# The weight pieces of an up-projection move to GpSimd, its gating to VectorE, and a half's first pieces move ahead of an attention output

## The chip, the cores and the metric

One core of one Trainium2 chip runs the whole program. The metric is the device time of one execution in microseconds (us). TensorE (PE in the profile) multiplies matrices, VectorE (DVE), ScalarE (ACT) and GpSimd (POOL) work element by element, and SyncE (SP) issues nearly all DMA transfers in one queue.

## The reference

One layer of a hybrid encoder over 2048 tokens of width 1024: a token mixer, a cross-attention into a memory, and the feed-forward block that this change is about.

```python
x = x + hybrid_token_mixer(rmsnorm(x, norm_mix), ...)
x = x + mem_cross_attn(rmsnorm(x, norm_x), memn, x_wq, x_wkv, x_wo)
h = rmsnorm(x, norm_ffn)
gate, val = split(h @ w_up)                   # 1024 -> 2 x 2816
gate = causal_dwconv(gate, conv_w, conv_b)    # 3 taps over the tokens
x = x + (silu(gate) * val) @ w_down           # 2816 -> 1024
return rmsnorm(x, norm_final)
```

## The kernel before

Every float32 matrix operand is used as a pair, a rounded high part and the remainder as low part; a product is three matmuls for each 128 rows (high x high, high x low, low x high). `resplit(t_, eng, raw)` makes a pair: ScalarE copies the high part (L1331), then the engine `eng` subtracts to get the low part (L1332).

The mixer fills the first 1400 us or so and is not touched. The rest is the block `attn_ffn`. It takes the tokens in two halves of 1024, each half as two blocks (NB = 2) of TB = 512 tokens. For each half, `attention` runs the scores and then `attn_out` for o = 0 and o = 1. One call of `attn_out` loops over 8 output tiles d; each loads two weight tiles `wvo` (L1286) and the residual `x2` (L1341), runs 24 matmuls, adds the residual on VectorE (L1344), stores it (L1345), and sums its squares (L1220: with o = 0 on GpSimd, with o = 1 on VectorE). With o = 1 it also makes the seven activation operands that the up-projection wants, `11`, `21`, `22`, `t1` to `t4`; the low parts of `t2` and `22` and four subtractions for `t4` (L1375) are GpSimd's.

Then `ffn_up` loops over 22 column tiles f. Both blocks and both halves of the rows of a weight tile are multiplied by a scheme with seven products in place of eight; each product is 12 matmuls (L1446 to L1448), so that an f has 84. The seven weight pieces are `a11`, `s1`, `s2`, `a12`, `s3`, `s4`, `a22`. With half 0, `up_weights` makes them from two raw tiles (`wraw`, two `load_raw` of 512 KB, L96): four sums s1 to s4 (L1426, L1428, L1430, L1432) and seven `resplit`; each piece is also stored in `ws_dram` (L1435). With half 1 the seven pieces are loaded from `ws_dram` (L1411) and nothing is formed. The `s` pieces lie in a pool of 7 buffers (`KQ`), which the attention uses for `wvo`; the `a` pieces have buffers of their own.

The products end in PSUM. ScalarE copies three of them to SBUF (`kept`, L1452: p1, p5, u2, and with `u3` a fourth). `gate(b)`, once for each block, is the chain of one f: copy of two carried columns (L1473), addition (L1474, one operand in PSUM), multiplication by the row scale `bc3` (L1475), ScalarE's first tap (L1476), two taps (L1478), copy of the new carry (L1479), tanh (L1481, into `fth`), its product (L1482), and a second multiplication by `bc3` (L1483). `u3 += p5` is L1489. The last products, L1499, take `u3` for one block and a PSUM tile `pd` for the other. `bc3` comes out of `bcast_rstd`: TensorE sums squares (`ssps`, L1226), the reciprocal root goes over VectorE and GpSimd (L182, L183), TensorE spreads it (`bcB`, L1235). `ffn_down` follows.

The block is put in order by a scheduler that simulates time with prices of its own (`schedule_with_timeline_sim=True`, L1183); each engine then works its list in order. A changed line can therefore move others.

Of the kernel before, what the change touches and what calls it, by code (L numbers as in the profile page):

```python
# [13 lines left out]
F32 = mybir.dt.float32  # L14
# [7 lines left out]
P = 128  # L22
# [34 lines left out]
def tile_hybrid_encoder(ctx: ExitStack, tc: tile.TileContext, t_in: dict, out: bass.AP, stage: str = "all"):  # L57
# [1148 lines left out]
    def KQ(shape, name):  # L1206
        return kq.tile(list(shape), FR, tag="kq", name=name)
# [193 lines left out]
    fcar = [fcars[:, 4 * f:4 * f + 2] for f in range(NFF)]  # L1401
    def up_weights(hf, f):

        H = KT // 2
        pcs = {}

        def piece(i, name):
            pool = name[0] == "a"
            pcs[name] = wpool.tile([P, 2, H, P], FR, tag="whl", name="wa", bufs=WB) if pool else KQ((P, 2, H, P), "ws")
            if hf:  # L1410
                nc.sync.dma_start(pcs[name].bitcast(F32), ws_dram[f, i])  # L1411
            return pcs[name]

        order = ("a11", "s1", "s2", "a12", "s3", "s4", "a22")
        if hf:
            for i, name in enumerate(order):
                piece(i, name)
            return pcs
        rg, rv = load_raw(t_in["f_up"][f]), load_raw(t_in["f_up"][NFF + f])
        g1, g2, v1, v2 = rg[:, :H], rg[:, H:], rv[:, :H], rv[:, H:]  # L1420
        s1r, s2r, s3r, s4r = [t_[:, u] for t_ in [K4((P, 2, H, P), "sr", F32) for _ in range(2)] for u in range(2)]
        raws = dict(a11=g1, a12=g2, a22=v2, s1=s1r, s2=s2r, s3=s3r, s4=s4r)
        for i, name in enumerate(order):
            t_ = piece(i, name)
            if name == "s1":
                nc.gpsimd.tensor_tensor(s1r, v1, v2, ALU.add)  # L1426
            elif name == "s2":
                nc.vector.tensor_tensor(s2r, s1r, g1, ALU.subtract)  # L1428
            elif name == "s3":
                nc.vector.tensor_tensor(s3r, v1, g1, ALU.subtract)  # L1430
            elif name == "s4":
                nc.gpsimd.tensor_tensor(s4r, g2, s2r, ALU.subtract)  # L1432
            resplit(t_, nc.vector if name in ("s2", "s3") else nc.gpsimd, raws[name])
            if S > HALF:
                nc.sync.dma_start(ws_dram[f, i], t_.bitcast(F32))  # L1435
        return pcs

    def ffn_up(hf, st, B, early):

        H = KT // 2  # L1440
        for f in range(NFF):
            w = up_weights(hf, f)

            def prod(ps, a, b, more=False):
                for k in range(H):
# [24 lines left out]
            def gate(b):  # L1470
                u = us[:, b]
                gt_ = T((P, TB + 2), "gt_")
                nc.gpsimd.tensor_copy(gt_[:, 0:2], fcar[f])  # L1473
                nc.vector.tensor_tensor(gt_[:, 2:], (R, Z)[b], (p1, u2)[b], ALU.add)  # L1474
                nc.vector.tensor_tensor(gt_[:, 2:], gt_[:, 2:], st[b]["bc3"], ALU.mult)  # L1475
                nc.scalar.activation(u, gt_[:, 2:], AF.Identity, scale=V("fcw2", f), bias=V("fcb", f))  # L1476
                for tap in range(2):
                    nc.vector.scalar_tensor_tensor(u, gt_[:, tap:tap + TB], V(f"fcw{tap}", f), u, ALU.mult, ALU.add)  # L1478
                nc.gpsimd.tensor_copy(fcar[f], gt_[:, TB:TB + 2])  # L1479
                th = T(name="fth")  # L1480
                nc.scalar.activation(th, u, AF.Tanh, scale=0.5)  # L1481
                nc.vector.scalar_tensor_tensor(u, th, 1.0, u, ALU.add, ALU.mult)  # L1482
                nc.gpsimd.tensor_tensor(u, u, st[b]["bc3"], ALU.mult)  # L1483

            if f:
                gate(0)
            prod(X, "s3", "t3", True)
            u3 = kept(X, "u3")
            nc.gpsimd.tensor_tensor(u3, u3, p5, ALU.add)  # L1489
            prod(Z, "s4", "22", True)  # L1490
            if f == 0:
                prod(X, "a22", "t4", True)
# [195 lines left out]
```

## Time and profile before

| | |
|---|---|
| median of 3 runs (lowest to highest) | 3439.07 us (3436.12 to 3439.97) |
| the profiled execution, its span | 3434.74 us, 3433.0 us |
| TensorE busy | 3242.5 us, 94% |
| VectorE busy | 2038.0 us, 59% |
| ScalarE busy | 1300.0 us, 38% |
| GpSimd busy | 1283.5 us, 37% |
| mean granted TensorE clock | 0.979 |

The profile is one execution; busy shares are means over stages with different limits, so the stretches of the up-projection are read on their own. The up-projection of half 0 fills about 1697 to 2197 us, that of half 1 about 2740 to 3190 us.

### The profile page before, as it was taken

What the parts mean: (1) busy time and instruction counts of PE and PEld (TensorE: products, weight loads), DVE (VectorE), ACT (ScalarE), POOL (GpSimd) and SP (SyncE); (2) the same over time, 40 slices, a digit from 0 to 9 for tenths busy, and PEclk for the clock granted to TensorE, in tenths of its full rate; (3) what the DMA queues carried; (4) which work ended last, traced back from release to release, by engine and by line L of the source; (5) the groups of instructions that cost most, each with busy time, mean ns of one, the idle gap of its engine ahead of it and who ended that gap; (6) DMA issues with size and microseconds to landing.
All of it is one profiled execution on the core that took longest, in us unless ns stands there. A gap on an engine that the chain in (4) does not pass through costs nothing.

```text
span 3433.0 us, 48215 instructions
## 1 busy us (share of the span) xinstructions
PE 3242.5 (94%) x16860; PEld 2646.4 (77%) x16860; DVE 2038.0 (59%) x3942; ACT 1300.0 (38%) x2593; POOL 1283.5 (37%) x1318
## 2 busy tenths in 40 slices
PE   6999999999999989899889999899999999999998
PEld 4777787788778778688677777687888778888787
DVE  5887777777777785343487777723243454445321
ACT  5445433543443345432234344433322232223432
POOL 5333121211211123531277777755611132323543
PEclk9999999999999999999999999999999999999999
DMA  5555444544444447866566666754556766666552
GB/s 206 210 180 183 142 142 130 176 131 142 147 131 128 131 128 233 270 209 213 177 238 237 241 240 245 258 185 158 172 199 203 236 212 218 219 222 214 194 173 76
DMA packets 317299, 647.72 MB, mean 189 GB/s; under 512 B 89728, under 2 KB 121600, under 8 KB 317056
## 3 DMA queue, kind: packets, MB, share of 16 engines
q1 hardware_dynamic: 312832, 642.53, 55.7%
q8 instruction: 134, 2.20, 0.3%
q10 hardware_dynamic: 4224, 2.10, 0.2%
q14 instruction: 109, 0.89, 0.1%
HBM read 454.64 MB, written 189.86 MB: 188 GB/s over the span
## 4 chain that ended last, share of the span: by engine, by line
PE 55%; DVE 15%; DMA 9%; POOL 8%; issue 8%; ACT 4%; SPq 1%; POOLq 0%; DVEq 0%; ACTq 0%
PE pd L147 11%; PE pd L1446 4%; PE pd L1447 4%; PE pd L1448 4%; DMA x<-x_dram 4%; PE dps L1547 3%; PE dps L1545 3%; PE dps L1546 3%; PE qy L147 2%; PE pd L176 2%; PE pd L173 2%; PE pd L175 2%; PE sc L1298 2%; PE sc L1300 2%; PE sc L1299 2%
## 5 line engine op out<-in xcount | busy, mean ns | idle before, releaser
L147 PE MATMUL pd<-hA,whl 128*128 128x512 f32 x2976 | 814.5, 411 | 16.1 <-ACT whl L121 7.8
L147 PEld LDWEIGHTS pd<-hA,whl 128*128 128x128 f32 x2976 | 535.6, 192 | 119.9 <-ACT whl L121 9.4
L1446 PE MATMUL pd<-h,ws 128*128 128x512 f32 x704 | 280.7, 402 | 46.5 <-ACT u L1452 30.4
L1332 POOL TENSOR_TENSOR wd<-wdr,wd 128x512 fp32r<-128x512 f32 x176 | 238.3, 1363 | 186.6 <-ACT wd L1331 186.5
L1545 PE MATMUL dps<-act,wd 128*128 128x512 f32 x704 | 275.8, 392 | 7.2 <-DVE x L1569 3.8
L1448 PE MATMUL pd<-h,ws 128*128 128x512 f32 x704 | 280.9, 400 | 0.8 <-POOL ws L1332 0.8
L1447 PE MATMUL pd<-h,ws 128*128 128x512 f32 x704 | 280.6, 399 | 0.0
L1546 PE MATMUL dps<-act,wd 128*128 128x512 f32 x704 | 275.4, 391 | 0.0
L124 POOL TENSOR_TENSOR whl<-wraw,whl 128x512 fp32r<-128x512 f32 x137 | 187.2, 1377 | 235.4 <-ACT whl L121 226.7
L1547 PE MATMUL dps<-act,wd 128*128 128x512 f32 x704 | 270.6, 392 | 4.6 <-POOL wd L1332 4.6
L1446 PE MATMUL pd<-h,wa 128*128 128x512 f32 x528 | 207.3, 396 | 9.6 <-ACT u L1452 9.6
L1447 PE MATMUL pd<-h,wa 128*128 128x512 f32 x528 | 207.1, 392 | 0.0
L1448 PE MATMUL pd<-h,wa 128*128 128x512 f32 x528 | 207.0, 392 | 0.0
L1446 PEld LDWEIGHTS pd<-h,ws 128*128 128x128 f32 x704 | 135.8, 193 | 83.5 <-ACT u L1452 38.0
L1331 ACT CAST wd<-wdr 128x512 fp32r<-128x512 f32 x176 | 107.7, 619 | 186.3 <-PE dps L1547 127.4
L1483 POOL TENSOR_TENSOR fu<-fu,bcs 128x512 f32<-128x512 f32 x88 | 132.2, 1502 | 102.3 <-DVE fu L1482 92.2
L1448 PEld LDWEIGHTS pd<-h,ws 128*128 128x128 f32 x704 | 135.8, 193 | 33.2 <-POOL ws L1332 4.6
L1545 PEld LDWEIGHTS dps<-act,wd 128*128 128x128 f32 x704 | 132.9, 189 | 36.2 <-ACT wd L1331 4.3
L1547 PEld LDWEIGHTS dps<-act,wd 128*128 128x128 f32 x704 | 132.5, 189 | 33.8 <-POOL wd L1332 6.3
L1447 PEld LDWEIGHTS pd<-h,ws 128*128 128x128 f32 x704 | 135.9, 193 | 28.5 <-DVE h L1332 0.4
L1546 PEld LDWEIGHTS dps<-act,wd 128*128 128x128 f32 x704 | 133.0, 189 | 27.7
L1332 DVE TENSOR_TENSOR act<-act 128x512 fp32r<-128x512 f32 x88 | 73.7, 860 | 108.7 <-ACT act L1331 107.6
(1034 smaller groups left out, 7368.1 us busy)
## 6 DMA issues: line engine op xcount, KB each, us to landing
whl<-w_split SPq DMA_DIRECT2D x186, 512.0 KB
ws_dram<-ws SPq DMA_DIRECT2D x88, 512.0 KB
wdr<-f_down SPq DMA_DIRECT2D x176, 256.0 KB
ws<-ws_dram SPq DMA_DIRECT2D x88, 512.0 KB
ws_dram<-wa SPq DMA_DIRECT2D x66, 512.0 KB
wa<-ws_dram SPq DMA_DIRECT2D x66, 512.0 KB
wqk<-qk_dram SPq DMA_DIRECT2D x64, 512.0 KB
wvo<-vo_dram SPq DMA_DIRECT2D x64, 512.0 KB
```

Of the source, the lines that this page charges most:

```text
L124: (nc.vector if dve else nc.gpsimd).tensor_tensor(t_[:, 1], r_, t_[:, 0].bitcast(F32), ALU.subtract)
L147: nc.tensor.matmul(out_, lhsT, rhs, **kw)
L173: nc.tensor.matmul(ps, hi[:, k % 4, :], a[:, 0, :n], start=(k == 0), stop=False)
L1331: nc.scalar.copy(t_[:, 0], raw)
L1332: eng.tensor_tensor(t_[:, 1], raw, t_[:, 0].bitcast(F32), ALU.subtract)
L1446: nc.tensor.matmul(ps, w[a][:, 0, k, :], B[b][k][:, 0, :], start=(k == 0 and not more), stop=False, skip_group_check=True)
L1447: nc.tensor.matmul(ps, w[a][:, 0, k, :], B[b][k][:, 1, :], start=False, stop=False, skip_group_check=True)
L1448: nc.tensor.matmul(ps, w[a][:, 1, k, :], B[b][k][:, 0, :], start=False, stop=(k == H - 1), skip_group_check=True)
L1483: nc.gpsimd.tensor_tensor(u, u, st[b]["bc3"], ALU.mult)
L1545: nc.tensor.matmul(pss[i], w[:, 0, i, :], a[:, 0, :], start=(f == 0), stop=False)
L1546: nc.tensor.matmul(pss[i], w[:, 0, i, :], a[:, 1, :], start=False, stop=False)
L1547: nc.tensor.matmul(pss[i], w[:, 1, i, :], a[:, 0, :], start=False, stop=(f == NFF - 1))
```

## The change

Three things. (a) All work on the weight pieces, four sums and seven low parts for each f of half 0, is GpSimd's (L1429 and L1332 of the new file); before, VectorE had s2, s3 and the low parts of both. (b) In the gating of both halves the two multiplications L1483 and the addition L1489 go from GpSimd to VectorE (new L1482 and L1488), and the four small copies L1473 and L1479 go to ScalarE. (c) `up_weights` returns a function `make` that makes chosen pieces; between `attn_out(o = 0)` and `attn_out(o = 1)` it makes `a11`, `s1`, `s2`, `a12` of the half's first f (with half 1 it loads them). Other lines of the new file are one or a few numbers off: matmuls L1445 to L1447, L1474 for L1475, L1477 for L1478, L1481 for L1482, L1498 for L1499.

```diff
-    def attention(st, toks):
+    def attention(st, toks, first):
...
                 for o in range(NB):
+                    if o:
+                        first(("a11", "s1", "s2", "a12"))
                     attn_out(st[o], o, B, ...)
...
-        for i, name in enumerate(order):
-            t_ = piece(i, name)
-            if name == "s1":
-                nc.gpsimd.tensor_tensor(s1r, v1, v2, ALU.add)
-            elif name == "s2":
-                nc.vector.tensor_tensor(s2r, s1r, g1, ALU.subtract)
-            elif name == "s3":
-                nc.vector.tensor_tensor(s3r, v1, g1, ALU.subtract)
-            elif name == "s4":
-                nc.gpsimd.tensor_tensor(s4r, g2, s2r, ALU.subtract)
-            resplit(t_, nc.vector if name in ("s2", "s3") else nc.gpsimd, raws[name])
...
+        def make(names=order):
...
+                if name[0] == "s":
+                    a, b, op = dict(s1=("a21", "a22", ALU.add), s2=("s1", "a11", ALU.subtract),
+                                    s3=("a21", "a11", ALU.subtract), s4=("a12", "s2", ALU.subtract))[name]
+                    nc.gpsimd.tensor_tensor(raws[name], raws[a], raws[b], op)
+                resplit(t_, nc.gpsimd, raws[name])
...
-                nc.gpsimd.tensor_copy(gt_[:, 0:2], fcar[f])
+                nc.scalar.copy(gt_[:, 0:2], fcar[f])
...
-                nc.gpsimd.tensor_copy(fcar[f], gt_[:, TB:TB + 2])
+                nc.scalar.copy(fcar[f], gt_[:, TB:TB + 2])
...
-                nc.gpsimd.tensor_tensor(u, u, st[b]["bc3"], ALU.mult)
+                nc.vector.tensor_tensor(u, u, st[b]["bc3"], ALU.mult)
...
-            nc.gpsimd.tensor_tensor(u3, u3, p5, ALU.add)
+            nc.vector.tensor_tensor(u3, u3, p5, ALU.add)
```

The first place is VectorE in the middle of half 0. Before, from the second multiplication of one block's gating to the last product of the f:

```order
L1430 TENSOR_TENSOR sr_18528<-wraw_18525,wraw_18523 128x512
L1478 SCALAR_TENSOR_TENSOR fu_18455<-gt__18456,vec_68,fu_18455 128x512
L1499 SCALAR_TENSOR_TENSOR fu_18292<-fu_18292,pd_18235 128x512
L1478 SCALAR_TENSOR_TENSOR fu_18455<-gt__18456,vec_68,fu_18455 128x512
L1428 TENSOR_TENSOR sr_18527<-sr_18527,wraw_18523 128x512
L1482 SCALAR_TENSOR_TENSOR fu_18455<-fth_18464,fu_18455 128x512
L1332 TENSOR_TENSOR ws_18538<-sr_18527,ws_18538 128x512
L1332 TENSOR_TENSOR ws_18547<-sr_18528,ws_18547 128x512
L1474 TENSOR_TENSOR gt__18495<-pd_18399,u2_18441 128x512
L1475 TENSOR_TENSOR gt__18495<-gt__18495,bcs_17828 128x512
```

VectorE there now, over the same part of an f (here `fu_18781`):

```order
L1477 SCALAR_TENSOR_TENSOR fu_18781<-gt__18782,vec_68,fu_18781 128x512
L1498 SCALAR_TENSOR_TENSOR fu_18618<-fu_18618,pd_18561 128x512
L1477 SCALAR_TENSOR_TENSOR fu_18781<-gt__18782,vec_68,fu_18781 128x512
L1481 SCALAR_TENSOR_TENSOR fu_18781<-fth_18790,fu_18781 128x512
L1482 TENSOR_TENSOR fu_18781<-fu_18781,bcs_17336 128x512
L1473 TENSOR_TENSOR gt__18821<-pd_18725,u2_18767 128x512
L1474 TENSOR_TENSOR gt__18821<-gt__18821,bcs_17828 128x512
L1477 SCALAR_TENSOR_TENSOR fu_18781<-gt__18821,vec_68,fu_18781 128x512 x2
L1481 SCALAR_TENSOR_TENSOR fu_18781<-fth_18829,fu_18781 128x512
L1488 TENSOR_TENSOR u3_18806<-u3_18806,p5_18753 128x512
L1482 TENSOR_TENSOR fu_18781<-fu_18781,bcs_17828 128x512
L1498 SCALAR_TENSOR_TENSOR fu_18781<-fu_18781,u3_18806 128x512
```

The four operations on `sr` and `ws` are gone, and nothing stands in their place between a tap and the product with the tanh that follows it; L1482 (twice) and L1488 are new.

The second place is TensorE at the start of the up-projection of half 0. Before, after the 12 matmuls on `a11` (`wa_17699`); `ws_17703` is s1, `ws_17708` is s2, `wa_17713` is a12:

```order
L1448 MATMUL pd_17731<-h3_17233,wa_17699 128x512
L1226 MATMUL ssps_17829<-ones_70,sq_17308 128x1 x4
L1235 MATMUL bcB_17837<-ident_63,rstd_17834 128x128 x4
L1446 MATMUL pd_17732<-h3_17370,ws_17703 128x512
L1447 MATMUL pd_17732<-h3_17370,ws_17703 128x512
L1446 MATMUL pd_17733<-h3_17038,wa_17713 128x512
```

TensorE there now, after 12 matmuls each on `a11`, s1 and a12 (`wa_17294`); `ws_17289` is s2, `ws_17716` is s3:

```order
L1447 MATMUL pd_17733<-h3_17272,wa_17294 128x512
L1226 MATMUL ssps_17829<-ones_70,sq_17331 128x1 x4
L1445 MATMUL pd_17731<-h3_17399,ws_17289 128x512
...
L1447 MATMUL pd_17731<-h3_17678,ws_17289 128x512
L1235 MATMUL bcB_17837<-ident_63,rstd_17834 128x128 x4
L1445 MATMUL pd_17731<-h3_17396,ws_17716 128x512
```

`ssps` and `bcB`, which stood behind one product, now stand behind three and four.

The third place is GpSimd at that start. Before (`hr` are the subtractions for `t4`):

```order
L1375 TENSOR_TENSOR hr_17663<-h3_17038,h3_17376 128x512
L183 TENSOR_TENSOR rstd_17834<-rstd_17834,nhalf_72 128x4
...
L1375 TENSOR_TENSOR hr_17687<-h3_17272,h3_17655 128x512
L1426 TENSOR_TENSOR sr_17697<-wraw_17695 128x512
L1332 TENSOR_TENSOR ws_17703<-sr_17697,ws_17703 128x512
```

GpSimd there now (`sr_17717` holds the raw s3 and s4):

```order
L1375 TENSOR_TENSOR hr_17694<-h3_17116,h3_17492 128x512
...
L1375 TENSOR_TENSOR hr_17710<-h3_17272,h3_17678 128x512
L183 TENSOR_TENSOR rstd_17834<-rstd_17834,nhalf_72 128x4
L1429 TENSOR_TENSOR sr_17717<-wraw_17277,wraw_17275 128x512
L1429 TENSOR_TENSOR sr_17717<-wraw_17275,sr_17284 128x512
L1332 TENSOR_TENSOR ws_17716<-sr_17717,ws_17716 128x512
```

The root `rstd`, which stood behind the first of the four subtractions, stands behind all of them, and the sums of s3 and s4 behind it.

The fourth place is SyncE's queue between `attn_out(o = 0)` and `attn_out(o = 1)` of half 0. Before (`wvo_17275` is the first weight tile of o = 1, `x2_17240` the last residual of o = 0):

```order
L1286 DMA wvo_17275<-vo_dram_79 128x1024
L1345 DMA x2_dram_15463<-x2_17123 128x512
L1341 DMA x2_17162<-x1_dram_15462 128x512
...
L1286 DMA wvo_17421<-vo_dram_79 128x1024
L1345 DMA x2_dram_15463<-x2_17240 128x512
L1341 DMA x2_17279<-x1_dram_15462 128x512
```

SyncE's queue there now (`wvo_17298` is the first weight tile of o = 1, `ws_17283` the piece s1):

```order
L1345 DMA x2_dram_15463<-x2_17240 128x512
L1341 DMA x2_17302<-x1_dram_15462 128x512
L1286 DMA wvo_17298<-vo_dram_79 128x1024
L1286 DMA wvo_17300<-vo_dram_79 128x1024
L1286 DMA wvo_17351<-vo_dram_79 128x1024
L1432 DMA ws_dram_15464<-ws_17283 128x1024
```

All weight tiles of o = 1 now stand behind the store of the last residual of o = 0.

## Rows read from the trace of the kernel before

**Rows 1.** Stretches: columns are us, then busy us (count) per engine, PEclk, DMA share, GB/s.

```profile
1700.00:1722.00 22.00, 4.68 (x18) 4.21 (x19) 18.80 (x24) 7.68 (x13) 12.88 (x10) 0.57 0.10 36
1780.00:2177.26 397.26, 365.10 (x1517) 290.02 (x1515) 310.96 (x289) 157.89 (x270) 302.25 (x253) 0.97 0.67 238
2800.00:3100.00 300.00, 300.00 (x1325) 248.48 (x1324) 140.81 (x187) 80.08 (x125) 84.71 (x109) 1.00 0.65 220
```

**Rows 2.** Waits, 1696 to 2200 us: engine, line and releaser; us in total, times, longest.

```profile
ACT fth L1481 <- DVE fu L1478: 77.8, 42, 2.2
DVE fu L1499 <- POOL u L1489: 51.7, 20, 2.7
...
PE pd L1446 <- ACT u L1452: 35.6, 31, 1.7
```

**Rows 3.** Timeline of VectorE, one f of half 0: start, us, operation, [idle before <-releaser].

```profile
1900.70 0.69 DVE L1482 SCALAR_TENSOR_TENSOR fu<-fth,fu 128x512 f32<-128x512 f32 x1 [0.70 <-ACT fth L1481]
1904.06 1.75 DVE L1499 SCALAR_TENSOR_TENSOR fu<-fu,u 128x512 f32<-128x512 f32 x1 [2.67 <-POOL u L1489]
...
1906.45 0.69 DVE L1475 TENSOR_TENSOR gt__19108<-gt__19108,bcs 128x512 f32<-128x512 f32 x1
1907.06 0.69 DVE L1430 TENSOR_TENSOR sr<-wraw 128x512 f32<-128x512 f32 x1
1908.03 1.56 DVE L1478 SCALAR_TENSOR_TENSOR fu<-gt__19108,vec,fu 128x512 f32<-128x512 f32 x1 [0.28 <-ACT fu L1476]
...
1910.11 1.18 DVE L1478 SCALAR_TENSOR_TENSOR fu<-gt__19108,vec,fu 128x512 f32<-128x512 f32 x1
1911.22 1.78 DVE L1428 TENSOR_TENSOR sr<-sr,wraw 128x512 f32<-128x512 f32 x1
1912.92 0.68 DVE L1482 SCALAR_TENSOR_TENSOR fu<-fth,fu 128x512 f32<-128x512 f32 x1
1913.68 3.29 DVE L1332 TENSOR_TENSOR ws<-sr,ws 128x512 fp32r<-128x512 f32 x2
...
1917.60 1.07 DVE L1475 TENSOR_TENSOR gt__19147<-gt__19147,bcs 128x512 f32<-128x512 f32 x1
1919.63 2.44 DVE L1478 SCALAR_TENSOR_TENSOR fu<-gt__19147,vec,fu 128x512 f32<-128x512 f32 x2 [0.96 <-ACT fu L1476]
1922.78 0.69 DVE L1482 SCALAR_TENSOR_TENSOR fu<-fth,fu 128x512 f32<-128x512 f32 x1 [0.70 <-ACT fth L1481]
```

**Rows 4.** Timeline of GpSimd in the same f.

```profile
1902.73 1.30 POOL L1489 TENSOR_TENSOR u<-u,p 128x512 f32<-128x512 f32 x1
...
1910.71 1.74 POOL L1332 TENSOR_TENSOR ws<-sr,ws 128x512 fp32r<-128x512 f32 x1
```

**Rows 5.** Groups of VectorE, 1780 to 2180 us: busy, mean ns, idle before.

```profile
L1499 DVE SCALAR_TENSOR_TENSOR fu<-fu,pd 128x512 f32<-128x512 f32 x18 | 12.1, 675 | 0.0
```

**Rows 6.** Timeline of VectorE, one f of half 1.

```profile
2912.44 0.69 DVE L1474 TENSOR_TENSOR gt__26550<-pd,p 128x512 f32<-128x512 f32 x1 [4.98 <-PE pd L1448]
...
2931.47 0.69 DVE L1474 TENSOR_TENSOR gt__26689<-pd,p 128x512 f32<-128x512 f32 x1 [4.98 <-PE pd L1448]
```

**Rows 7.** Groups of ScalarE, whole span: its smallest operation.

```profile
L1311 ACT ACTIVATION_READ_ACCUMULATOR pr<-sc,smax,scl 128x1 f32 x64 | 12.8, 200 | 0.0
```

**Rows 8.** Timeline of TensorE, start of the up-projection of half 0.

```profile
1705.40 1.87 PE L1226 MATMUL ssps<-ones,sq 128*128 128x1 f32 x8 [6.02 <-DVE sq L1220]
1709.88 2.07 PE L1235 MATMUL bcB<-ident,rstd 128*128 128x128 f32 x8 [2.61 <-POOL rstd L183]
1721.26 0.79 PE L1446 MATMUL pd<-h,ws 128*128 128x512 f32 x1 [9.31 <-ACT ws L1331]
```

**Rows 9.** Timeline of GpSimd at that start.

```profile
1708.44 1.38 POOL L183 TENSOR_TENSOR rstd<-rstd,nhalf 128x4 f32<-128x4 f32 x1 [0.70 <-DVE rstd L182]
...
1713.06 4.15 POOL L1375 TENSOR_TENSOR hr<-h,h 128x512 f32<-128x512 f32 x3
```

**Rows 10.** Timeline of all engines: a 512 KB load's issue, its first reader.

```profile
1727.57 0.38 SPq L96 DMA_DIRECT2D wraw<-f_up  x1
...
1732.25 0.62 ACT L1331 CAST wa<-wraw 128x512 fp32r<-128x512 f32 x1 [1.53 <-DMA wraw<-f_up]
```

More of the change, by code (lines that the diff above doesn't have):

```diff
@@ L1404, in up_weights @@
         H = KT // 2
[L1405 to L1412, printed above, removed]
+        pcs, raws = {}, {}
         order = ("a11", "s1", "s2", "a12", "s3", "s4", "a22")
-        if hf:
+        def make(names=order):
+            if not hf and not raws:
+                rg, rv = load_raw(t_in["f_up"][f]), load_raw(t_in["f_up"][NFF + f])
+                raws.update(a11=rg[:, :H], a12=rg[:, H:], a21=rv[:, :H], a22=rv[:, H:])
@@ L1416, in up_weights @@
             for i, name in enumerate(order):
[L1417 to L1422, printed above, removed]
-        for i, name in enumerate(order):
-            t_ = piece(i, name)
-            if name == "s1":
-                nc.gpsimd.tensor_tensor(s1r, v1, v2, ALU.add)
-            elif name == "s2":
-                nc.vector.tensor_tensor(s2r, s1r, g1, ALU.subtract)
-            elif name == "s3":
-                nc.vector.tensor_tensor(s3r, v1, g1, ALU.subtract)
-            elif name == "s4":
-                nc.gpsimd.tensor_tensor(s4r, g2, s2r, ALU.subtract)
-            resplit(t_, nc.vector if name in ("s2", "s3") else nc.gpsimd, raws[name])
-            if S > HALF:
-                nc.sync.dma_start(ws_dram[f, i], t_.bitcast(F32))
@@ L1436, in up_weights @@
-        return pcs
-    def ffn_up(hf, st, B, early):
+                if name not in names or name in pcs:
+                    continue
+                t_ = pcs[name] = (wpool.tile([P, 2, H, P], FR, tag="whl", name="wa", bufs=WB) if name[0] == "a"
+                                  else KQ((P, 2, H, P), "ws"))
+                if hf:
+                    nc.sync.dma_start(t_.bitcast(F32), ws_dram[f, i])
+                    continue
+                if name in ("s1", "s3"):
+                    r2 = K4((P, 2, H, P), "sr", F32)
+                    raws[name], raws["s2" if name == "s1" else "s4"] = r2[:, 0], r2[:, 1]
@@ new lines, in make, with ffn_up @@
+                if name[0] == "s":
[3 more added lines that the diff above has]
+                resplit(t_, nc.gpsimd, raws[name])
+                if S > HALF:
+                    nc.sync.dma_start(ws_dram[f, i], t_.bitcast(F32))
+        return pcs, make
+    def ffn_up(hf, st, B, first, early):
@@ L1440, in ffn_up @@
         H = KT // 2
         for f in range(NFF):
-            w = up_weights(hf, f)
+            w, make = first if f == 0 else up_weights(hf, f)
+            make()
             def prod(ps, a, b, more=False):
@@ L1579, in tile_hybrid_encoder @@
         toks = [hf * HALF + b * TB for b in range(NB)]
-        B = attention(st, toks)
+        first = up_weights(hf, 0)
+        B = attention(st, toks, first[1])
         nxt = []
@@ L1587, in tile_hybrid_encoder @@
         D = Down(hf)
-        ffn_up(hf, st, B, D.early)
+        ffn_up(hf, st, B, first, D.early)
         ffn_down(hf, D, ahead)
```

## The prediction

> **What bounds the kernel now.** I read the stretches first. In half 1's up-projection, 2800 to 3100 us, TensorE is busy for 300.00 of 300.00 us, and VectorE and GpSimd for 140.81 and 84.71: TensorE is the bound, and work that moves between the other engines is covered [rows 1]. In half 0's, 1780 to 2177 us, TensorE is busy for 365.10 of 397.26 us, with VectorE at 310.96 and GpSimd at 302.25: something else paces it. From 1700 to 1722 us TensorE is nearly idle (4.68 of 22.00) [rows 1]. So the change can pay at the start of half 0's up-projection and in its 22 f's, and hardly elsewhere.
>
> Next, the waits and one f. VectorE's L1482 recurs at 1900.70 and 1922.78: a period of 22.08 us [rows 3]. In half 1, where TensorE paces, L1474 recurs at 2912.44 and 2931.47: 19.03 us, which is what 84 matmuls cost [rows 6]. So at most 3.05 us an f, 20 x 3.05 = 61 us over the 20 steady f's (the first and the last differ), can come from the steady part. VectorE's two largest idle causes in half 0 are the addition of u3 by GpSimd (51.7 us, 20 times, 2.67 in the f shown) and the chain tap, tanh, product [rows 2, 3]. TensorE's largest is ScalarE's copy of u2 out of PSUM (35.6 us, 31 times) [rows 2].
>
> **What VectorE sheds in a steady f.** Off it go L1430 (0.69), L1428 (1.78) and the two low parts (3.29): 5.76 us. The wait of 2.67 for GpSimd's u3 goes too, since u3 is now added on VectorE itself [rows 3]. Together 8.43.
>
> **What it takes on.** Three operations with two operands in SBUF, the two second multiplications and the u3 addition. Bounds for one: 0.69, as L1475, and 1.75, as L1499 with u3, which ran while GpSimd ran [rows 3]. I take 1.25, just above the mean of the nine that stay (L1475 0.69 and 1.07, L1478 1.56, 1.18 and 2.44, L1482 0.69 and 0.68, L1499 1.75: 10.06 / 9 = 1.12), since GpSimd will be denser: 3.75 (bounds 2.1 and 5.3). Gaps also open that the weight work filled. L1430 lay before a tap, L1428 and the low parts between a tap and the next product. In the other block, where nothing fills them, the same gaps are 0.96 against 0.28 and 0.70 against none [rows 3]: 0.68 + 0.70 = 1.38.
>
> **What the moved weight work does to the others.** GpSimd goes from ten operations of full size and four small copies an f to eleven of full size and none. A GpSimd operation is 1.30 alone and 1.74 beside VectorE [rows 4], so eleven are 14.3 to 19.1 us: no bound of its own over 19.1. It runs ahead as far as buffers allow, so it is nearly always at work, and the nine operations that stay on VectorE grow. From 1.12 to 1.25 is 1.2 us (bounds 0, and 9 x (1.75 - 1.12) = 5.7).
>
> What distinguishes quick from slow rows is where the operands lie: L1499 with `pd` in PSUM has a mean of 0.675 over 18 [rows 5], L1499 with u3 in SBUF took 1.75 [rows 3]. [...]
>
> ScalarE takes four copies of 2 columns. Its smallest row is 200 ns [rows 7], so 0.8 us an f, on an engine busy for 157.89 of 397.26 us [rows 1]: nothing by itself. But its list has the tanh ahead of copies that free PSUM, so part of the waits of TensorE remains. Those were 35.6 us, 1.8 for each of 20 f's [rows 2]; the taps and tanhs that hold the copies up come somewhat earlier now, so I leave 1.1 of it as a new term on the chain (bounds 0 and 1.8).
>
> **Sum for a steady f:** 22.08 - 8.43 + 3.75 + 1.38 + 1.2 + 1.1 = 21.1 us. The gain is 1.0 x 20 = 20 us. With the low bounds the sum is below 19.03, so TensorE sets it and the gain is about 55 to 60; with the high ones, all at once, it is 22.08 - 8.43 + 5.3 + 1.38 + 5.7 + 1.8 = 27.8; rival 2 prices the same contention at one mean.
>
> [...]
>
> **The start of half 0's up-projection.** TensorE idles 6.02 us before the sums of squares, 2.61 before `bcB` and 9.31 before its first matmul on s1, together 17.9 [rows 8]. Now a11, s1, a12 and s2 are there and can run while VectorE and GpSimd finish the activations. Two things take the place of the wait. L183, the root that `bcB` needs, ran at 1708.44 and now stands behind the four subtractions, of which three took 4.15 us until 1717.21 [rows 9]; and GpSimd forms s3 and s4 only behind it, four operations of 1.3 to 1.7, so s3's matmuls with the low part hardly run before 1722. s1, a12 and s2 are 36 matmuls, 36 / 84 x 19.03 = 8.2 us at full clock. I take 9 us gained: these matmuls, and the little that comes earlier (bounds 3, if s2 waits for GpSimd's low part of t2, and 15). The 22 us around that place have a granted clock of 0.57 [rows 1], the lower of two levels in large part, after TensorE's idling; more matmuls there may lift it, and that is inside the upper bound.
>
> **The boundary of half 0.** SyncE's queue holds the first weight tile of o = 1 behind the store of o = 0's last residual; before, weight tiles were issued ahead of it. TensorE then waits for a load that is as large as one of `wraw`: issue at 1727.57, first reader at 1732.25, 4.7 us [rows 10]. Behind it the clock may be low for some matmuls. I take 5 lost (bounds 2, part hidden behind VectorE's last additions, and 10). What is queued behind: all other weight tiles, and the store of s1, which waits for GpSimd's low part.
>
> **Half 1** has neither: the pieces come by load, and take two places among the weight tiles that are issued early. Its up-projection has TensorE busy throughout [rows 1]; three more VectorE operations of 0.69 on an engine at 47% are covered by it: 0. If that cover failed, by a wait at the end of each gating chain, it would be at most the 3 x 0.69 = 2 us an f, which I find far.
>
> **Sum.** -20 - 9 + 5 = -24 us on the profiled execution's 3434.74: 3410.7. The median of the runs lies 4.33 above the profiled execution, so the forecast is **3415**.
>
> **Rivals.**
> 1. *TensorE becomes the bound.* The VectorE operations stay near 0.7 to 1.1, the ScalarE waits go: 19.1 to 19.4 us an f, gain 54 to 59; with the start and the boundary 3439 - 57 - 9 + 5 = 3378 (3370 to 3388). For it: VectorE's sheds are real, 8.43. Against: GpSimd is back to back.
> 2. *Slower: VectorE's chain meets GpSimd at every other step.* The twelve operations have a mean of 1.5 in place of 1.25, midway between quiet and the 1.75 of L1499 and up: 12 x 1.5 + 3 x 0.68 + the four gaps of 0.70 and 0.96 (3.3) = 23.3 us an f [rows 3, 5]; 20 x 1.25 = +25, -9 + 5: 3460 (3446 to 3480). By the same count the mean of 1.25 gives 20.3, before the 1.1. It decides from a mean of 1.41, or 1.32 with the 1.1: there the period is 22.3, and the steady part eats what the start gives. For it: GpSimd always at work, and L1428, the low parts and L1499 at 1.65 to 1.78. Against: GpSimd runs only 11 an f, and rows beside it stand at 1.07 and 1.18 too.
> 3. *The wait only changes its name.* The period stays at 22, set by ScalarE's list (tanh ahead of the copies of p5 and u2, and seven high parts), and the start gives 9 less 5: 3435 (3432 to 3439).
> 4. *The first pieces do not help:* the wait for s1 goes and `bcB` and s3 are as late as before; the start gives 0 to 3 and the boundary costs 5 to 10. With the steady gain, 3421 to 3425; it is inside the forecast's own range of 3396 to 3430.
>
> **How the numbers follow.** Forecast with rival 4 0.50, rival 1 0.16, rival 3 0.16, rival 2 0.18. A difference below 0.2%, 6.9 us, cannot be told from none here. Faster: forecast and rival 1, 0.66. Same: rival 3, 0.16. Slower: rival 2, 0.18. The range reaches from inside rival 1 to the lower part of rival 2, 3382 to 3450, and leaves out about 2 in 10.
>
> **What would show it.** Right: no idle before VectorE's product with u3; L1474 to L1482 of new at means of 1.1 to 1.4; a period of 20.5 to 21.5; the wait for s1 gone, with one for `rstd` or s3 of some 5 us in its place; TensorE waiting once for `wvo` near 1600 us. Wrong: twelve VectorE operations at 1.7 (rival 2); a TensorE share near 100% in half 0 (rival 1); half 1's period off 19.03.

## The result, and the profile after

The changed kernel takes 3419.45 us (median; 3414.17 to 3421.99), the kernel before 3439.07; the ratio is 0.9942, 95% interval 0.9925 to 0.996. The profiled execution takes 3414.17 us with a span of 3412.5, 20.5 less than the span before. The forecast of 3415 held as a sum, and that was luck. Its terms did not hold: the gain lies at the start of the up-projections, and hardly any of it in the steady f's (an f is one of the 22 column tiles; a steady one has the same order of instructions as its neighbours).

The stretches (columns as in [rows 1]), same windows:

```profile
1700.00:1722.00 22.00, 16.98 (x72) 13.75 (x72) 19.27 (x24) 8.42 (x17) 14.67 (x10) 0.91 0.12 41
1780.00:2177.26 397.26, 358.71 (x1516) 292.91 (x1515) 313.83 (x279) 169.19 (x352) 319.17 (x201) 0.94 0.65 243
2800.00:3100.00 300.00, 300.00 (x1325) 248.43 (x1324) 162.33 (x238) 86.94 (x191) 0.00 (x0) 1.00 0.65 221
```

At the start of half 0's up-projection TensorE is busy for 16.98 of 22 us, where it was 4.68, and its granted clock is 0.91 there, where it was 0.57. In the middle it is busy for 358.71 us, less than the 365.10 before. GpSimd rose from 302.25 to 319.17 there, VectorE stayed (313.83 against 310.96). In half 1 GpSimd is empty and TensorE full, as before.

Where the time went, from the starts of TensorE's first matmul of each stage in the two traces (us):

| stage | before | after | difference |
|---|---|---|---|
| up to the attention outputs of half 0 (untouched code) | 1601.7 | 1603.7 | +2.0 |
| the two attention outputs of half 0 | 94.9 | 99.3 | +4.5 |
| up-projection of half 0, to its last matmuls | 519.2 | 498.3 | -20.9 |
| down-projection, attention of half 1 | 425.4 | 426.8 | +1.4 |
| the two attention outputs of half 1 | 93.6 | 96.8 | +3.2 |
| up-projection of half 1 | 443.7 | 437.5 | -6.2 |
| to the end | 254.5 | 250.1 | -4.4 |

(Before, half 0's up-projection ends at 2215.7 us, and not at about 2197: the first matmuls of the down-projection start while the last f is unfinished.)

The 20.9 us of half 0 split by VectorE's last product with `pd`, once for each f: to that of the first f -20.8 (58.5 to 37.7 from the first matmul), over the next three f's +3.7, over the next seventeen -2.5, at the end -1.3.

The waits in half 0's up-projection:

```profile
ACT fth L1480 <- DVE fu L1477: 88.5, 41, 3.9
POOL wa L1332 <- ACT wa L1331: 53.4, 24, 5.8
...
PE pd L1445 <- ACT p L1451: 41.0, 8, 5.8
```

The wait of VectorE for GpSimd's u3 (51.7 us in [rows 2]) is gone, and TensorE's for `u` copies (35.6) is down to 1.8. In their place stands one kind of wait, 8 times and 41.0 us in all: TensorE for the copy of a `p` tile. ScalarE's list shows why. The rows are start, duration, operation and the idle time before it with what ended it:

```profile
1898.49 0.81 ACT L1475 ACTIVATE fu<-gt__19108,vec 128x512 f32<-128x512 f32 x1 [3.87 <-DVE gt__19108 L1474]
...
1903.52 0.63 ACT L1480 ACTIVATE fth<-fu 128x512 f32<-128x512 f32 x1 [3.60 <-DVE fu L1477]
1904.05 0.18 ACT L1472 COPY gt__19147<-fcar 128x2 f32<-128x2 f32 x1
1904.13 0.58 ACT L1451 COPY p<-pd 128x512 f32<-128x512 f32 x1
```

The copy at 1904.13 (p5 of one f) stands behind the first tap L1475 and the tanh L1480 of the same f, and these wait 3.87 and 3.60 us for VectorE. TensorE meanwhile:

```profile
1904.76 0.80 PE L1445 MATMUL pd<-h,ws 128*128 128x512 f32 x1 [5.80 <-ACT p L1451]
1905.36 0.63 PE L1446 MATMUL pd<-h,ws 128*128 128x512 f32 x1
```

It idles 5.80 us, and the matmuls behind that idle time take 0.63 us, where those ahead of it took 0.39. The stretch behind it, and the next (columns as in [rows 1]):

```profile
1904.70:1910.50 5.80, 5.74 (x16) 4.56 (x17) 1.40 (x3) 3.30 (x7) 5.19 (x5) 0.61 0.97 330
1910.50:1916.00 5.50, 5.50 (x26) 4.56 (x25) 4.45 (x6) 3.06 (x7) 2.94 (x2) 1.00 0.99 387
```

The granted clock is 0.61 on average over 5.8 us: 0.50 until 1909.2 us, and 1.00 from 1909.3 on. This comes once in three f's, since the order of the lists now repeats only after three. VectorE over such three f's (a few of its rows; the first and the last are the same instruction three f's apart):

```profile
1900.07 3.41 DVE L1477 SCALAR_TENSOR_TENSOR fu<-gt__19108,vec,fu 128x512 f32<-128x512 f32 x2
...
1914.69 0.69 DVE L1488 TENSOR_TENSOR u<-u,p 128x512 f32<-128x512 f32 x1
...
1916.20 0.69 DVE L1482 TENSOR_TENSOR fu<-fu,bcs 128x512 f32<-128x512 f32 x1
...
1935.86 1.77 DVE L1482 TENSOR_TENSOR fu<-fu,bcs 128x512 f32<-128x512 f32 x1
...
1951.81 1.78 DVE L1482 TENSOR_TENSOR fu<-fu,bcs 128x512 f32<-128x512 f32 x1
...
1955.21 1.78 DVE L1488 TENSOR_TENSOR u<-u,p 128x512 f32<-128x512 f32 x1
...
1965.40 3.41 DVE L1477 SCALAR_TENSOR_TENSOR fu<-gt__19597,vec,fu 128x512 f32<-128x512 f32 x2
```

65.33 us for three f's are 21.78 for one, where 22.08 was measured before [rows 3]. The second multiplication L1482 takes 0.69 in one f and 1.77 in the next, and L1488 0.69 and 1.78: in these three f's they took 0.69 where GpSimd was idle at their start and 1.18 to 1.78 where it worked. Two of GpSimd's rows in these three f's:

```profile
1911.66 1.77 POOL L1332 TENSOR_TENSOR wa<-wraw,wa 128x512 fp32r<-128x512 f32 x1
...
1935.34 1.74 POOL L1332 TENSOR_TENSOR wa<-wraw,wa 128x512 fp32r<-128x512 f32 x1
```

The first ends at 1913.43 and nothing follows it for some us, so that L1488 at 1914.69 and L1482 at 1916.20 run alone (0.69); the second lies beside L1482 at 1935.86 (1.77).

### The profile page after: what moved, and what is told of

Read it like the earlier page. It is cut to its first block, busy times and chain, and to the rows that moved or that the text cites. A ratio compares the mean times of both kernels' runs of the same rounds, so it can differ in the third digit from the quotient of the medians.

```text
span 3412.5 us, 47946 instructions
## 1 busy us (share of the span) xinstructions
PE 3230.2 (95%) x16860; PEld 2642.5 (77%) x16860; DVE 2059.9 (60%) x3986; ACT 1317.4 (39%) x2769; POOL 1182.9 (35%) x1098
## 4 chain that ended last, share of the span: by engine, by line
PE 60%; DVE 16%; issue 7%; DMA 7%; POOL 5%; ACT 3%; SPq 1%; POOLq 0%; DVEq 0%; ACTq 0%
PE pd L147 11%; PE pd L1445 6%; PE pd L1446 6%; PE pd L1447 6%; PE pd L176 2%; PE pd L173 2%; PE dps L1546 2%; PE dps L1544 2%; PE dps L1545 2%; POOL wd L1332 2%; PE pd L175 2%; PE qy L147 2%; DVE fu L1477 2%; DMA x<-x_dram 2%; PE sc L1298 2%
## 5 line engine op out<-in xcount | busy, mean ns | idle before, releaser
L1332 POOL TENSOR_TENSOR wd<-wdr,wd 128x512 fp32r<-128x512 f32 x176 | 245.4, 1403 | 596.8 <-ACT wd L1331 586.7
L1445 PE MATMUL pd<-h,ws 128*128 128x512 f32 x704 | 280.7, 402 | 48.2 <-ACT p L1451 42.5
L1447 PE MATMUL pd<-h,ws 128*128 128x512 f32 x704 | 278.3, 397 | 0.0
L1445 PE MATMUL pd<-h,wa 128*128 128x512 f32 x528 | 205.6, 390 | 1.5 <-ACT u L1451 1.5
L1447 PE MATMUL pd<-h,wa 128*128 128x512 f32 x528 | 205.6, 389 | 0.4 <-POOL wa L1332 0.4
L1445 PEld LDWEIGHTS pd<-h,ws 128*128 128x128 f32 x704 | 136.5, 194 | 82.5 <-ACT p L1451 46.4
L1447 PEld LDWEIGHTS pd<-h,ws 128*128 128x128 f32 x704 | 136.0, 193 | 29.5 <-POOL ws L1332 0.4
L1332 POOL TENSOR_TENSOR ws<-sr,ws 128x512 fp32r<-128x512 f32 x88 | 140.7, 1616 | 17.4 <-ACT ws L1331 17.4
L1332 DVE TENSOR_TENSOR act<-act 128x512 fp32r<-128x512 f32 x88 | 70.5, 819 | 111.3 <-ACT act L1331 104.5
```

Of the source, the lines that this page charges most:

```text
L1332: eng.tensor_tensor(t_[:, 1], raw, t_[:, 0].bitcast(F32), ALU.subtract)
L1445: nc.tensor.matmul(ps, w[a][:, 0, k, :], B[b][k][:, 0, :], start=(k == 0 and not more), stop=False, skip_group_check=True)
L1447: nc.tensor.matmul(ps, w[a][:, 1, k, :], B[b][k][:, 0, :], start=False, stop=(k == H - 1), skip_group_check=True)
```

## The experiments

The lists of VectorE and ScalarE in the middle of half 0 repeat, in all runs but one (early pieces and weights, below). On ScalarE, with "hi" for a cast of a weight piece, "act" for L1475 and "th" for the tanh, three patterns occur:

```
A  p5 hi act hi hi th hi hi u2 hi act hi th u3 p1                (the kernel before)
B  u2 hi act hi th hi hi u3 act hi p1 hi th hi p5                (third part alone, and others)
C  three f's long; p5, u2 ahead of a tanh in one f, behind it in the next   (the changed kernel)
```

In some runs with list B one "hi" stands a place earlier, and with C the list can be five f's long; where that is so, the text says it. Ratios below are against runs of the kernel before on the same chip. Parts are named as in the section on the change: (a) weight pieces on GpSimd, (b) gating on VectorE and copies on ScalarE, (c) first pieces early.

**Without the early pieces.** (a) and (b).

```diff
-                        first(("a11", "s1", "s2", "a12"))
+                        pass
```

> The change without its third part: nothing is made or loaded between the two attention outputs; weight pieces on GpSimd and gating on VectorE as changed. Theory A (the gain sits at the start of each up-projection, the steady f's gave only 0.3 us each, 22.07 to 21.77): about 3439 - 6 - 4 = 3429 (3424 to 3434), the wait of some 9 us before the first s1 matmul of half 0 is back, and no wait for a first weight tile between the attention outputs. Theory B (the forecast's sum: the steady f's give 20): about 3419, no slower than the changed kernel.

3424.28 us, ratio 0.9963 (0.9946 to 0.998). The f's are as in the changed kernel (29.8, 18.5 and 16.7 us, list C), the first product of half 0 comes 58.8 us after its first matmul, as before the change (58.5). Theory A holds: the early start is (c)'s, and (a) with (b) gives little in the steady f's. The early start does not last, though: the next three f's take 59.6 us here and 69.9 in the changed kernel, and the intervals of the two ratios overlap.

**The early pieces alone.** (c), on the old engines.

```diff
-                    nc.gpsimd.tensor_tensor(raws[name], raws[a], raws[b], op)
-                resplit(t_, nc.gpsimd, raws[name])
+                    (nc.vector if name in ("s2", "s3") else nc.gpsimd).tensor_tensor(raws[name], raws[a], raws[b], op)
+                resplit(t_, nc.vector if name in ("s2", "s3") else nc.gpsimd, raws[name])
...
-                nc.scalar.copy(gt_[:, 0:2], fcar[f])
+                nc.gpsimd.tensor_copy(gt_[:, 0:2], fcar[f])
```

(and likewise the other copy, the second multiplication and the u3 addition back to GpSimd)

> The third part alone: a half's first pieces ahead of its last attention output; every sum, low part and gating step on the engine that had it before. Theory A: up-projection of half 0 some 12 to 17 us shorter at its start, attention output 4.5 longer, steady f near 22: about 3439 - 15 + 5 = 3429 (3422 to 3434). Theory B: the start gives 9 and the boundary takes 5: 3435 (3432 to 3439).

3399.29 us, ratio 0.9888 (0.9865 to 0.9912): twice the gain of the whole change, and neither theory had it. The steady f fell to 20.0 us although no engine's share of the work differs from the kernel before. ScalarE's list is B, where the copy of u2 stands ahead of the tanh. The waits, same columns as [rows 2]:

```profile
DVE fu L1498 <- POOL fu L1482: 31.8, 22, 3.6
...
PE pd L1445 <- ACT u L1451: 13.5, 19, 3.5
```

TensorE waits 13.5 us for `u` copies, where it was 35.6, and VectorE 31.8 for GpSimd ahead of its last products, where it was 51.7. The matmul that waits tells which copy it is: the product behind u2's copy takes an `s` piece (s3), that behind u3's an `a` piece (a22). Before, 29.2 us of the 35.6 lay ahead of an `s` piece and 6.3 ahead of an `a` piece, so the forecast's reading of all of it as u2's was nearly right. Here the 13.5 are all u3's: the wait for u2 is gone.

**s1 and s2 of the first f in other buffers.**

```diff
-... if name[0] == "a"
+... if name[0] == "a" or (f == 0 and name in ("s1", "s2"))
```

> The changed kernel, but s1 and s2 of a half's first f lie in the buffers of the a pieces, so that the weight tiles of the last attention output keep all their 7 buffers. If the buffers taken from them cost the 4.5 us (half 0) and 3.2 us (half 1) by which the attention outputs grew: 4 to 8 us faster than the changed kernel, about 3413. If those came from the store and the residual in the queue, or from GpSimd's work, no change: 3419.

3425.22 us, ratio 0.9957 (0.9946 to 0.9968): not faster. The attention outputs did shrink, 95.9 us (half 0) and 93.6 (half 1), and the wait for a weight tile between them, in the changed kernel

```profile
1657.03 0.77 PE L173 MATMUL pd<-pt,wvo 128*128 128x512 f32 x1 [2.43 <-DMA wvo<-vo_dram]
```

is gone. So the buffers taken from the weight tiles did make that wait. But TensorE waits elsewhere for as long. In half 0

```profile
1722.38 0.79 PE L1445 MATMUL pd<-h,wa 128*128 128x512 f32 x1 [10.45 <-ACT p L1451]
```

for the copy of p1, behind one more cast of an activation in ScalarE's list than in the changed kernel; in half 1 for an activation, and then for the load of a piece:

```profile
2739.30 0.79 PE L1445 MATMUL pd<-h,wa 128*128 128x512 f32 x1 [7.94 <-ACT h L1331]
...
2751.92 0.80 PE L1445 MATMUL pd<-h,wa 128*128 128x512 f32 x1 [5.07 <-DMA wa<-ws_dram]
```

That load is issued at 2744.32, in the changed kernel at 2734.19. The four buffers of the `a` pieces are all taken until then, which would explain it; that was not tried by itself. The up-projection of half 1 takes 449.1 us in place of 437.5: the gain was given back.

**p5 copied by VectorE.**

```diff
-            p5 = kept(Z, "p5")
+            p5 = TQ(name="p5")
+            nc.vector.tensor_copy(p5, Z)
```

> The changed kernel, but VectorE copies p5 out of PSUM instead of ScalarE. Theory A (in one f of three ScalarE's list holds a first tap and a tanh ahead of that copy, and TensorE idles 5.8 us and then runs some 2.4 us longer at the low clock): three f's take 65.3 - 8 + up to 3 = 57 to 60 us, 3419 less 35 to 50 for the 18 f's concerned: 3375 to 3390. Theory C (VectorE's own chain beside GpSimd sets the pace, and the wait shows there only): three f's stay at 64 to 66 us, 3415 to 3425, and TensorE waits for another copy or for VectorE.

3416.34 us, ratio 0.9936 (0.9911 to 0.996), f's of 29.8, 18.5 and 16.7 us: no change. Theory A as I had put it, that this copy is the matter, falls, and what theory C had forecast is there: 65.0 us for three f's, and TensorE waiting for something else of ScalarE's:

```profile
PE pd L1445 <- ACT ws L1331: 38.9, 8, 5.9
...
PE pd L1445 <- ACT p L1451: 3.3, 1, 3.3
```

The same 8 waits of up to 5.9 us are there, now for the cast of a weight piece that stands behind the same tanh. What delays TensorE is the tap and the tanh in ScalarE's list, whatever stands next behind them, and they wait for VectorE.

**Only a11 early, on the old engines.** As the early pieces alone, with

```diff
-                        first(("a11", "s1", "s2", "a12"))
+                        first(("a11",))
```

> The kernel with the old split of the work, and of a half's first pieces only a11 made or loaded between the two attention outputs. VectorE's and ScalarE's lists in the middle of half 0 are then those of the kernel before, not those of the third part alone. Theory D (the third part brought the steady f from 22.07 to 20.0 us because the scheduler, started with s1 at hand, lays another repeating order, with the copy of u2 ahead of the tanh): f's at 22.0 to 22.1 us, in all 3432 to 3442. Theory E (the earlier start itself carries through, whatever the order): f's below 21, in all below 3425.

3435.97 us, ratio 0.9986 (0.9971 to 1.0001); 22.07 us an f, list A. The waits are those of the kernel before:

```profile
DVE fu L1498 <- POOL u L1488: 51.7, 20, 2.7
...
PE pd L1445 <- ACT u L1451: 38.1, 33, 1.7
```

Theory D holds here: without s1 at hand the scheduler lays the old order, and the period is the old one. With the run on the early pieces alone, this says that 2.07 us an f hang on the order of the lists, at the same split of the work.

**Early pieces and gating, weights as before.** (b) and (c): in the changed kernel only the sums and low parts of s2 and s3 back on VectorE, the first four lines of the diff of the early pieces alone.

> The second and the third part of the change without the first: weight pieces formed as in the kernel before, the gating on VectorE and the small copies on ScalarE, first pieces early. ScalarE's list in the middle is that of the third part alone. Theory D (the order sets the period): 20.0 us an f, 3395 to 3403. Theory F (VectorE's load beside GpSimd sets it; three more operations of 0.7 to 1.75, less the wait of 1.4 for GpSimd's product): 20.7 to 22 us, 3413 to 3440. With part one on top, the changed kernel, it was 21.8.

3386.66 us, ratio 0.9833 (0.9806 to 0.986), the fastest of all; 19.4 us an f, near the 19.03 at which TensorE is full. List B, but for the place of one cast. The middle, columns as in [rows 1], here over 360 us:

```profile
1780.00:2140.00 360.00, 358.52 (x1559) 289.66 (x1558) 337.80 (x353) 161.92 (x350) 185.34 (x131) 1.00 0.71 268
```

VectorE is busy for 337.80 of 360 us (310.96 of 397.26 before [rows 1]), and GpSimd for half. Both theories had more. So part (a), on top of (b) and (c), costs 33 us by the medians (3419.45 against 3386.66) and some 37 by the ratios.

**The early pieces, and only the small copies on ScalarE.** (c), with L1472 and L1478 on ScalarE.

> The third part alone, and the four small copies of an f on ScalarE instead of GpSimd (2.4 us an f off GpSimd, 0.7 onto ScalarE). Theory F (VectorE and GpSimd, each busy for some 87% of an f of 20.0 us, set the period): 19.1 to 19.7 us an f, 3380 to 3393. Theory D: unchanged at 20.0 unless ScalarE's list turns bad, 3395 to 3403.

3414.91 us, ratio 0.9918 (0.9894 to 0.9942); 20.8 us an f, slower than (c) alone by 0.8 though GpSimd has less to do. Both theories missed. The copy of u3, which stood ahead of the second first-tap, stands behind it in this list, and TensorE waits more for `u` copies than the 13.5 us above:

```profile
PE pd L1445 <- ACT u L1451: 25.7, 20, 2.4
```

**Early pieces and weights, gating as before.** (a) and (c).

> The first and the third part without the second: GpSimd forms all weight pieces and keeps its gating steps and copies, 14 operations of 1.3 to 1.74 and four copies of some 0.6 an f. Theory F: GpSimd sets the period, 14 x 1.3 + 2.4 = 20.6 to 14 x 1.74 + 2.4 = 26.8 us, taken 24: about 3475 (3440 to 3520). Theory D (order alone): it could stay near 20 to 22, 3400 to 3435.

3437.65 us, ratio 0.9995 (0.9979 to 1.0012); f's of 18.9 to 27.2 us, 22.4 on average, and no repeating list. GpSimd is full:

```profile
1780.00:2140.00 360.00, 324.82 (x1366) 256.73 (x1366) 232.41 (x197) 143.46 (x247) 357.96 (x294) 0.99 0.62 238
```

357.96 of 360 us. Theory F had the bound right and its size too high: GpSimd's 14 operations took 1.5 us each, and its four copies 0.4 where 0.6 was taken, 22.6 us in all.

**Half of (a): the low parts of s2 and s3 on GpSimd.** As (b) and (c), with

```diff
-                resplit(t_, nc.vector if name in ("s2", "s3") else nc.gpsimd, raws[name])
+                resplit(t_, nc.gpsimd, raws[name])
```

> The second and third part of the change and half of the first: the low parts of s2 and s3 on GpSimd (9 full operations an f there), their sums on VectorE (14 with two operands in SBUF). ScalarE's repeating list is that of the run with parts two and three. Theory D (the order of ScalarE's list, copies of u2 ahead of the tanh or not, sets the period): 19.1 to 19.6 us an f, 3380 to 3392. Theory F (it is how full GpSimd is, since VectorE's operations wait behind its): between 19.4 with 7 and 21.8 with 11 operations, 20.2 to 20.8, 3400 to 3413.

3391.92 us, ratio 0.9863 (0.9847 to 0.988); 20.3 us an f with ScalarE's list B unchanged. That is F's number for the f (20.2 to 20.8), while the total lies below F's 3400 to 3413 and at the end of D's 3380 to 3392. The f decides, since the theories are about it, and D had 19.1 to 19.6. The middle:

```profile
1780.00:2140.00 360.00, 348.45 (x1495) 277.57 (x1494) 338.27 (x303) 155.28 (x336) 244.68 (x160) 1.00 0.68 258
```

VectorE has two operations an f less than in the run with (b) and (c) and is busy for as long (338.27 us): those with both operands in SBUF take 1.28 us on average, where they took 1.07.

**The other half of (a): the sums of s2 and s3 on GpSimd.** The same counts on each engine, but ScalarE's list is of kind C, five f's long.

> As the run before, but the other half: the sums of s2 and s3 on GpSimd, their low parts on VectorE. The counts of operations are the same, 9 and 14, but ScalarE's list changes from f to f as in the changed kernel, with p5 behind a tanh in some. Theory D: 21 to 22 us an f on average, 3410 to 3425. Theory F: as with the low parts, whatever that gave, within 0.3 us an f.

3433.93 us, ratio 0.9979 (0.9966 to 0.9992); f's of 15.4 to 29.8 us, 22.3 on average. Two us an f more than its twin at the same load, so F alone cannot be right. Not all of it is the order of ScalarE's copies, though; raw tiles were late as well:

```profile
ACT wa L1331 <- DMA wraw<-f_up: 28.7, 6, 6.0
PE pd L1445 <- ACT u L1451: 26.6, 13, 4.1
```

**Gating alone.** (b).

> The second part alone: gating on VectorE, small copies on ScalarE, no early pieces, weight pieces formed as before. ScalarE's list is that of the kernel before (u2 behind a tanh). Theory D: TensorE still waits for u2 in each f, 21 to 22 us, 3420 to 3435. Theory F: GpSimd has 7 operations, so 19.4 to 20 us an f as in the run with parts two and three, and only the old start is back: 3395 to 3410.

3391.46 us, ratio 0.9864 (0.9849 to 0.9878); 20.4 us an f with list A, as before the change. So with ScalarE's order held, moving three operations and the small copies off GpSimd is worth 1.7 us an f. D's 21 to 22 falls, F's 19.4 to 20 is nearly met, and the total is below both, since half 1 gained as well (its up-projection took 436.8 us). The middle:

```profile
1780.00:2140.00 360.00, 341.82 (x1483) 276.66 (x1483) 326.76 (x337) 155.84 (x336) 185.63 (x124) 1.00 0.68 258
```

**s1 alone in other buffers, on (b) and (c).**

```diff
-... if name[0] == "a"
+... if name[0] == "a" or (f == 0 and name == "s1")
```

> Parts two and three, with s1 of a half's first f in a buffer of the a pieces, so that the weight tiles of the last attention output keep 6 of their 7 buffers in place of 5, and a fourth a buffer stays free for a22. If the buffers make the waits for weight tiles: 2 to 5 us faster than parts two and three, 3381 to 3385. If the a buffers hold up the next pieces, as they did with both s1 and s2 there: 2 to 8 us slower.

3391.66 us, ratio 0.9862 (0.9842 to 0.9883); (b) and (c) had 0.9833 (0.9806 to 0.986). The intervals overlap, so this settles nothing; a gain is not seen. The attention outputs took 99.8 us in half 0 and 99.1 in half 1, against 100.9 and 95.5.

## Why the sum held, and which steps did not

The runs side by side. The mean is that of VectorE's operations with both operands in SBUF, from its timeline of 1800 to 2120 us; GpSimd's count is of full operations an f. B' is B with one cast a place earlier.

| run | us an f | ScalarE's list | GpSimd, an f | VectorE with two in SBUF, an f | mean us |
|---|---|---|---|---|---|
| before | 22.1 | A | 10 | 13 | 1.22 |
| (c) | 20.0 | B | 10 | 13 | 1.25 |
| (c), small copies on ScalarE | 20.8 | B', u3 behind a tap | 10 | 13 | 1.32 |
| (b) | 20.4 | A | 7 | 16 | 1.08 |
| (b), (c) | 19.4 | B' | 7 | 16 | 1.07 |
| (b), (c), low parts | 20.3 | B' | 9 | 14 | 1.28 |
| (b), (c), sums | 22.3 | C | 9 | 14 | 1.18 |
| (a), (c) | 22.4 | none repeats | 14 | 9 | 1.40 |
| (a), (b), (c), the change | 21.8 | C | 11 | 12 | 1.27 |

Part (a) can be read off three pairs of runs: (c) without and with it, 0.9888 and 0.9995; (b), 0.9864 and 0.9963; (b) and (c), 0.9833 and 0.9942. Each time it costs 34 to 38 us of the 3439, whatever else is there. (a) alone was not run.

**What bounds it.** Right: TensorE in half 1, whose f stayed at 19.0 us; in half 0 a chain over VectorE and ScalarE.

**What VectorE sheds and takes on.** Right in its sizes. The wait for u3 went, and the twelve operations that are left have a mean of 1.27 us; the forecast took 1.25.

**The sum for a steady f.** This step failed: 21.1 us was forecast, with 20.5 to 21.5 as its sign of being right, and 21.8 came, so that a gain of 20 us became some 3 to 6. The term that was mis-sized is the 1.1 us for ScalarE's waits, what was left of an old 1.8. TensorE loses 65.3 - 3 x 19.03 = 8.2 us in three f's, 2.7 an f: 5.8 of idle time in one place, 1.9 an f, and the low clock behind it, 0.8, which had no term. VectorE's 65.33 us show the same from its side: it waits 8.4 us for TensorE's products, 2.8 an f. Of the other terms, its work is 50.6 us, 16.9 an f, where the forecast's count in rival 2 gives 17.0 with the mean of 1.25, and its gaps behind ScalarE are 5.9 us, 2.0 an f, where that count has 3.3. Together that is 21.8 with the small gaps. The forecast had seen that the tanh stands ahead of copies, and had spread the wait evenly; it lies in one f of three, and the granted clock behind it was 0.50 for some 4.5 us. Rival 3, which kept the period at 22 and put it down to ScalarE's list, came closest on this term.

**What sets the period** is thus two things, and the forecast weighed only one. How full GpSimd is goes with how long VectorE's operations take: 1.07 to 1.08 us with 7 operations an f on GpSimd, 1.18 to 1.32 with 9 to 11, 1.40 with 14. With ScalarE's order held, it moves the period: 22.1 against 20.4 (before and (b)), 20.3 against 19.4 (with and without the low parts). The order of the lists sets how much of it reaches TensorE: 22.1 against 20.0 with the same split of the work (before and (c)), 22.3 against 20.3 with the same counts (the two halves of (a), with the late raw tiles as a second difference). Neither explains the table alone. That the order is the cause between before and (c) is shown by the run with a11 alone, which keeps the old order and the old period, and by the wait for u2, which is there with the one order and not with the other. No run set an order by hand, and why the scheduler lays one or the other was not traced.

In the changed kernel's rows the same L1482 of VectorE, with both operands in SBUF, took 0.69 us alone and 1.77 beside GpSimd, while L1498 with `pd` in PSUM took 0.67 beside it (at 1922.22). But the operations of full size in the table's two columns are 23 an f in every run, and the period goes from 19.4 to 22.4: their count alone tells nothing here. What matters, as I read the rows, is on whose path that time is lost: VectorE's operations are the chain that ScalarE and TensorE wait for, and GpSimd's pieces are made ahead. That reading is argued; no run tests it by itself.

**The start of half 0.** Mis-sized: 9 us forecast (bounds 3 to 15), 17.1 came over the first four f's, 20.8 to the first product. There are three waits again: the two that were forecast, for `rstd` and for s3, and one for the copy of a p tile:

```profile
1715.09 0.79 PE L1445 MATMUL pd<-h,ws 128*128 128x512 f32 x1 [2.98 <-ACT p L1451]
...
1721.55 2.07 PE L1235 MATMUL bcB<-ident,rstd 128*128 128x128 f32 x8 [2.05 <-POOL rstd L183]
1725.91 0.79 PE L1445 MATMUL pd<-h,ws 128*128 128x512 f32 x1 [2.29 <-ACT ws L1331]
```

They are 2.98, 2.05 and 2.29 us, in place of 6.02, 2.61 and 9.31 [rows 8]. L183 ran at 1720.04, behind the subtractions, as read from the order. The forecast counted 36 matmuls at full clock; it had left the clock to the upper bound, and that rose from 0.57 to 0.91 over these 22 us. Before, it was 1.00 from 1690 to 1702.5 us and 0.50 from 1705 to 1722; now it is 1.00 from 1700 to 1711, with the matmuls there. These are the two levels that the forecast speaks of: from 1590 to 2230 us of the trace before, 1152 of 1280 pieces of 0.5 us have 1.00 and 106 have 0.50. (Rival 4's own terms, 0 from the start and 10 lost at the boundary, reach 3429 and not 3425.)

**The boundary of half 0.** Right in sum: +5 forecast, +4.5 measured, with one wait for a first weight tile. That wait is 2.43 us, half of the load of 4.7 that was counted. Most of the rest had no term: TensorE's wait for GpSimd's squares ahead of the sums of squares (L1226) is 3.75 us where it was 2.21. In the three runs that make neither s1 nor s2 early that wait was 1.85 to 3.89 us and the whole stage 94.5 to 97.4, so a good part of the 4.5 may be chance. The cause given for the wait for the tile was half of it too: the tiles stand behind the residual's store because two of their buffers are gone, as the run with other buffers showed.

**Half 1.** Forecast 0, measured +3.2, -6.2 and -4.4. The start of its up-projection had a wait too, which I had not priced. Before:

```profile
2745.05 0.79 PE L1446 MATMUL pd<-h,ws 128*128 128x512 f32 x1 [5.40 <-ACT h L1331]
```

and after:

```profile
2731.55 0.49 PE L1445 MATMUL pd<-h,ws 128*128 128x512 f32 x1 [1.73 <-ACT h L1331]
```

5.40 us became 1.73, and the first matmul behind it 0.49 in place of 0.79. Neither the +3.2 nor the -6.2 is a firm number: in two runs without early pieces, (a) with (b) and (b) alone, whose code for half 1 is the same, the attention outputs took 92.4 and 97.5 us and the up-projection 445.4 and 436.6. The -4.4 goes with (b): the stretch to the end took 249 to 253 us in the nine kernels with (b) and 254 to 258 in the five without it. Where in that stretch it lies was not traced.

So the sum was right by luck: a steady gain that did not come (14 us or more short) was made up by a start that gave 8 more and by half 1, which had no term.

## What to carry to other kernels

Work that an idle engine makes ahead is not free where the operations of an engine that others wait for take longer beside it: here VectorE's with both operands in SBUF took 1.07 us on average with 7 operations an f on GpSimd and 1.27 with 11, and the same sums and low parts cost less on VectorE itself, then busy 94% of the time at 19.4 us an f, than on GpSimd at 21.8. Take a change of several parts apart even when it is faster: the weight pieces on GpSimd cost some 33 us, and without them the kernel takes 3386.66 us, faster than both kernels compared here. Where a scheduler orders the lists, a change that only starts a stage differently can move the whole stage by a tenth, so read the repeating order in the middle, instruction by instruction, for each engine, and ask of each wait what stands behind it.

## What was not expected of the hardware

A stall of TensorE cost more than its idle time. Behind 5.80 us of idle time the granted clock was 0.50 for some 4.5 us, 0.61 on average over 5.8, and a matmul took 0.63 us in place of 0.39. Of the 8.2 us lost in three f's 5.8 are the idle time, and the 2.4 that are left are that.

The untouched part ahead varies more between executions than several of the effects here: the first matmul of the projection behind the mixer came between 1407.4 and 1419.8 us in the profiled executions of the 14 kernels shown here, which all have the same code up to there. Lengths of stages, not totals, were compared for that reason.
